# Staging the vector and scalar work of the second layer's feed-forward, one product step apart

## The chip, the cores and the metric

One core of one Trainium2 chip runs the whole program. TensorE (PE in the profile) does the matrix products, VectorE (DVE), ScalarE (ACT) and GpSimd (POOL) the element-wise work, SyncE's queue (SP) issues the weight loads. Each engine takes its instructions in the order in which the program wrote them and waits at any whose inputs are not there. The metric is the device time of one execution in microseconds (us).

## What is computed

A backbone of two layers over 512 tokens of width 1024, with 256 context tokens in front. Each layer mixes tokens in four branches and ends with a feed-forward part. The change is in the feed-forward part of the second layer, where only the 512 latent tokens are left:

```python
def sq_relu_mlp(h, w1, w2):          # w1: 1024 x 4096, w2: 4096 x 1024
    return jnp.square(jax.nn.relu(h @ w1)) @ w2
...
x = x + gt2 * sq_relu_mlp(h2, w_ff1[l], w_ff2[l])
...
return rmsnorm(x, g_final)
```

## The kernel before

**Products in two parts.** A 32-bit operand is split into a high part (a copy on ACT, rounded to the matmul's type) and a low part (source minus high part, on DVE or POOL); a product is three matmuls: high by high, high by low, low by high. `split` issues the copy (L344) and right behind it the subtraction (L345).

**Seven products.** w_ff1 is worked off in 16 quarters, each 1024 x 256. The first three are plain. For the other 13 (`seven`), the eight half-size block products are replaced by seven, P1 to P7, over sums of blocks. Per quarter that takes four weight sums on DVE (`seven_weights`: L294 and L296 for P6, L299 for P7, L308 for P3), a high and a low part per product, five adds that read the products' PSUM banks (L1451 to L1471), three rectifiers on ACT (L1461, L1467, L1473), and two squares (L1480), each followed by a split of the result. The sums on the side of the activations are made once, by the thread `sums` (adds and subtractions at L1405 and L1408 on DVE, then splits), which other work interleaves with.

**The product list.** `mixed` first runs `ff1_first` (the first four tiles of w_ff1, each followed by `act`: rectifier L1330 on ACT, square L1332 on DVE, split), then `ff_order`'s list of 149 steps: F, a plain w_ff1 tile (24 matmuls of 128x512, twice); S, one of the seven products (12 matmuls of 128x256, 91 times); a, one output tile of w_ff2 (12 matmuls of 128x512, 56 times; an odd a shares the weights of the even one before it). The list begins FFaaaSaSSaSaSaSSA (the capital A ends a group of eight a) and then repeats 14 S and 8 a for two quarters; FF_LEAD (5.6 us) sets how many products of the next quarters run ahead of the a steps. `ff2_last` follows with the last w_ff2 tiles and the final norm.

**What sets the order on DVE and ACT.** At each step `w_ahead` issues, ahead of the step's own matmuls, the loads of all weights due within LOAD_US = 12 us of the list's time and the sums and splits of those due within SPLIT_US = 6 us. `split`, the bank reads, the rectifier and the square are issued as soon as the code reaches them, right behind the matmuls that feed them. A tile whose number divides by `pool_share` has its low part on POOL (three in this stage).

Of the kernel before, what the change touches and what calls it, by code (L numbers as in the profile page):

```python
# [9 lines left out]
F32 = mybir.dt.float32  # L10
BF16 = mybir.dt.bfloat16
F32R = mybir.dt.float32r
# [54 lines left out]
SPLIT_US, LOAD_US, FF_LEAD = 6.0, 12.0, 5.6  # L67
# [49 lines left out]
class Net:  # L117
# [44 lines left out]
    def plan(self):  # L162
        d = self.d
        items = []
        self.when, self.sevens = {}, {}
# [22 lines left out]
        for l in range(DEPTH):  # L188
# [10 lines left out]
            if l in STRASSEN:  # L199
                t = 0.0  # L200
                for kind, a, b, us in self.ff_order(l):
# [6 lines left out]
                    self.when[items[-1][0]] = self.when.get(items[-1][0], t)  # L208
                    t += us
# [38 lines left out]
    def w_advance(self, dma, split):  # L248
# [8 lines left out]
        while self.n_split < min(split + 1, len(self.items)):  # L257
            i = self.n_split
            if self.items[i][0][0] == "seven":
                self.wsp[i] = self.seven_weights(i, *self.items[i][0][1:])  # L260
                self.n_split += 1
                continue
# [16 lines left out]
    def seven_weights(self, i, l, q, j):  # L279
# [35 lines left out]
        return w  # L315

    def w_ahead(self, *key):

        i = self.n_got
        now = self.when[key]  # L320

        def until(us):
            j = i
            while j + 1 < len(self.items) and self.when.get(self.items[j + 1][0], now + us + 1.0) <= now + us:
                j += 1
            return j

        split, load = max(until(SPLIT_US), i + 1), until(LOAD_US)
        self.n_got += 1
        assert self.items[i][0] == key, (self.items[i][0], key)  # L330
# [933 lines left out]
    def out(self, l, groups, x, h):  # L1264
# [6 lines left out]
        held = []  # L1271

# [11 lines left out]
        for m in range(KT):  # L1284
            xo = sb.get([128, NTOK], F32, "xo")
            nc.gpsimd.dma_start(xo[:, :n], self.x_src[m][:, :n])
            x.append(xo)
# [31 lines left out]
    def ff(self, l, ranges, groups, x, h, na, nb, after, near):  # L1319
# [17 lines left out]
        def ff1_first():  # L1337
# [6 lines left out]
            self.until(*nb, KT - 1)  # L1344
            hid = [act((b,), groups[:1]) for b in banks]
# [15 lines left out]
        def ff2_one(c, m, w, hid, rngs):  # L1361
            banks = self.proj(w, [256 * k + 128 * (m % 2) for k in range(4)], hid, rngs, "f2")
            for (a, e), o in zip(rngs, banks):
                nc.vector.scalar_tensor_tensor(x[m][:, a:e], o[:, :e - a], self.modcol(l, int(a >= SEQ), 5, m),  # L1364
                                               x[m][:, a:e], op0=OP.mult, op1=OP.add)
            ps.free(*banks)
# [30 lines left out]
        def sums():  # L1397

            blocks = {n: [] for n in ("T1", "T2", "T3", "T4")}
            keep = []  # L1400
            for k in range(4):
                v = sb.get([128, 4, 256], F32, "v7", ph=True)
                for i in range(2):
                    hi, lo = (t[:, :512].bitcast(F32).rearrange("p (a b) -> p a b", a=2) for t in h[k + 4 * i])
                    nc.vector.tensor_tensor(v[:, 2 * i:2 * i + 2], hi, lo, op=OP.add)  # L1405
                    yield 0.7
                for o, a, b in ((0, 1, 0), (1, 3, 1), (3, 3, 0), (2, 2, 3)):
                    nc.vector.tensor_tensor(v[:, o], v[:, a], v[:, b], op=OP.subtract)  # L1408
                yield 1.0
                t = sb.get([128, 2, 2, 256], F32R, "T7", ph=True)  # L1410
                keep.append(t)
                for n, i, (hi, lo) in (("T2", 3, [z[:, 512:] for z in h[4 + k]]), ("T3", 1, (t[:, 0, 0], t[:, 0, 1])),
                                       ("T1", 0, [z[:, 512:] for z in h[k]]), ("T4", 2, (t[:, 1, 0], t[:, 1, 1]))):
                    blocks[n].append(self.split(v[:, i], "T7", hi, lo))
                    yield 0.6
                sb.free(v)
# [5 lines left out]
        def seven(q, hid):  # L1422
# [5 lines left out]
            u = sb.get([128, 256], F32, "u7", ph=True)  # L1428

            def product(j):  # L1430
                n = SEVEN[j]
                w = self.w_ahead("seven", l, q, j)
# [13 lines left out]

            b1, o1 = product(0)
            nc.scalar.activation(u, o1, AF.Copy)
# [439 lines left out]
```

## Time and profile before

| | us |
|---|---|
| median of 3 runs | 2201.86 (2199.62 to 2201.98) |
| profiled execution | 2200.57 |
| its span, first to last instruction | 2198.8 |
| product list, first F to first matmul of `ff2_last` | 361.4 (1800.51 to 2161.92) |

The profile is of one execution. PE is busy for 96% of the span, DVE for 66%, ACT for 38%. The product list is 16% of the span; everything before it and the code after it are the same in both kernels. A timeline row gives start, duration, engine, line and operation, output tile <- input tiles, and in brackets the idle time of the engine just before it with the instruction that ended the wait. "x12" is a run of 12 equal instructions; matmuls overlap, so a run's pace is read from one row's start to the next. PEclk is the granted TensorE clock, 1.0 for 2.4 GHz and 0.5 for 1.2 GHz.

### The profile page before, as it was taken

Reading aid. Unit: us, or ns where it says so; the run is one execution under the profiler, and the core shown is the slowest. Engines: PE = TensorE matmul, PEld = TensorE weight load, DVE = VectorE, ACT = ScalarE, POOL = GpSimd, SP = SyncE. Lnnn points to the kernel's source line nnn. Section 1 sums busy time; section 2 is a strip of 40 time slices with the busy share of each in tenths; the row PEclk is TensorE's granted clock in tenths of the full one; section 3 lists DMA queues with packets and bytes.
Section 4 is the critical chain, followed back from the end, with each engine's and each line's share of the span. In section 5 each row is a group of like instructions: output and inputs, shape, how many; then the busy total and the mean of one; then the engine's idle time right before and its main releaser. Section 6 shows DMA issues by size and latency. Waiting matters only on the chain. (4 is left out here: it accounts for less than half of the span.)

```text
span 2198.8 us, 30361 instructions
## 1 busy us (share of the span) xinstructions
PE 2110.1 (96%) x12168; PEld 1829.9 (83%) x12168; DVE 1451.1 (66%) x2434; ACT 829.9 (38%) x1391; POOL 441.3 (20%) x387
## 2 busy tenths in 40 slices
PE   8899999999999999999999999999999997989988
PEld 6788888888888888888888888888888986777877
DVE  6667657689874668877333475767875577566566
ACT  3455542233432432122221245554423343343434
POOL 2432210025431322122000134332000130000000
PEclk9999999999999999999999999999999999999999
DMA  7111122133433144456221212223323321222222
GB/s 299 44 61 54 49 76 85 44 120 125 134 116 134 49 149 169 152 201 230 68 68 49 86 39 77 68 68 113 123 86 97 124 68 58 87 87 77 77 86 77
DMA packets 62173, 218.45 MB, mean 99 GB/s; under 512 B 7248, under 2 KB 9312, under 8 KB 62032
## 3 DMA queue, kind: packets, MB, share of 16 engines
q1 hardware_dynamic: 45136, 155.21, 21.4%
q0 software_dynamic: 16896, 61.30, 8.1%
q8 instruction: 95, 1.56, 0.3%
q14 instruction: 46, 0.38, 0.1%
HBM read 212.29 MB, written 4.19 MB: 98 GB/s over the span
## 5 line engine op out<-in xcount | busy, mean ns | idle before, releaser
L345 POOL TENSOR_TENSOR wl<-wraw,wh 128x1024 fp32r<-128x1024 f32 x86 | 211.5, 2460 | 1249.3 <-ACT wh L344 885.9
L364 PE MATMUL f<-fh,wh 128*128 128x512 f32 (+1 forms) x1040 | 289.2, 353 | 0.9 <-ACT fh L344 0.4
L344 ACT ACTIVATE wh<-wraw 128x1024 fp32r<-128x1024 f32 x242 | 249.5, 1048 | 48.4 <-DVE wl L345 23.1
L364 PE MATMUL f<-h,wh 128*128 128x256 f32 (+1 forms) x1184 | 257.7, 333 | 0.0
L364 PE MATMUL f<-fh,wl 128*128 128x512 f32 (+1 forms) x800 | 243.4, 349 | 6.9 <-DVE wl L345 3.5
L345 DVE TENSOR_TENSOR wl<-wraw,wh 128x1024 fp32r<-128x1024 f32 x156 | 202.5, 1304 | 32.7 <-ACT wh L344 30.9
L364 PEld LDWEIGHTS f<-h,wh 128*128 128x128 f32 x1184 | 184.7, 188 | 24.2
L1364 DVE SCALAR_TENSOR_TENSOR xo<-f,mod,xo 128x512 f32<-128x512 f32 (+1 forms) x200 | 122.8, 639 | 112.1 <-PE f L364 111.9
L364 PEld LDWEIGHTS f<-fh,wh 128*128 128x128 f32 x1040 | 173.3, 188 | 26.3 <-ACT fh L344 0.7
L425 DVE CUSTOM_DVE_ANT_0 junk<-wm,silu,pp 128x1024 bf16<-128x1024 f32 x116 | 157.7, 1360 | 12.3 <-DMA wm<-w_mod 11.0
L364 PE MATMUL f<-h,wl 128*128 128x512 f32 (+1 forms) x592 | 161.8, 335 | 0.0
L364 PE MATMUL g<-h,wh 128*128 128x512 f32 x512 | 161.6, 393 | 0.0
L364 PEld LDWEIGHTS f<-fh,wl 128*128 128x128 f32 x800 | 134.7, 188 | 30.4 <-DVE wl L345 5.7
L364 PE MATMUL f<-fl,wh 128*128 128x512 f32 (+1 forms) x560 | 155.2, 342 | 0.0
L364 PE MATMUL g<-hh,wh 128*128 128x512 f32 (+1 forms) x512 | 131.9, 338 | 0.0
L364 PE MATMUL g<-hh,wl 128*128 128x512 f32 (+1 forms) x512 | 131.3, 337 | 0.6 <-DVE wl L345 0.6
L364 PE MATMUL g<-hl,wh 128*128 128x512 f32 (+1 forms) x512 | 131.6, 338 | 0.0
L1330 ACT ACTIVATE ft<-f 128x512 f32<-128x512 f32 (+1 forms) x74 | 32.4, 477 | 247.8 <-PE f L364 247.8
L747 DVE SCALAR_TENSOR_TENSOR ca<-z,pp,ca 128x783 f32<-128x783 f32 (+1 forms) x120 | 121.0, 1008 | 1.9
L1186 ACT ACTIVATE g<-g 128x512 f32<-128x512 f32 x96 | 46.9, 523 | 194.2 <-PE g L364 193.3
L364 PE MATMUL y<-br,wh 128*128 128x512 f32 x480 | 119.6, 357 | 0.3 <-DVE br L345 0.2
L1441 PEld LDWEIGHTS f<-h,w 128*128 128x128 f32 x780 | 108.4, 206 | 12.8 <-ACT w L344 6.5
(430 smaller groups left out, 4419.0 us busy)
## 6 DMA issues: line engine op xcount, KB each, us to landing
wraw<-w_ff SPq DMA_DIRECT2D x128, 512.0 KB, 3.6
wraw<-w_in SPq DMA_DIRECT2D x96, 512.0 KB, 3.5
wm<-w_mod POOLq DMA_DIRECT2D x80, 512.0 KB, 4.5
wm<-w_mod SPq DMA_DIRECT2D x16, 512.0 KB, 10.2
wraw<-w_out SPq DMA_DIRECT2D x16, 512.0 KB, 3.6
wraw<-w_v SPq DMA_DIRECT2D x8, 512.0 KB, 5.7
bias<-bias POOLq DMA_DIRECT2D x16, 256.0 KB, 3.0
wraw<-w_ba SPq DMA_DIRECT2D x8, 512.0 KB, 3.6
```

The costliest lines, as they stand in the source:

```text
L344: nc.scalar.activation(hi, src, AF.Copy)
L345: (eng or nc.vector).tensor_tensor(lo, src, hi.bitcast(F32), op=OP.subtract)
L364: self.nc.tensor.matmul(o[:, :t1 - t0], a[:, sl], b[:, t0:t1], start=start and a is wh and b is xh, stop=stop and a is wl)
L425: nc.vector.tensor_tensor_reduce(self.junk, w, self.silu[c], 1.0, b, OP.mult, OP.add, o)
L747: nc.vector.scalar_tensor_tensor(a[:, :n], zs[ct][:, j:j + n], w, a[:, :n], op0=OP.mult, op1=OP.add)
L1186: nc.scalar.activation(g[:, a:e], o[:, :e - a], func, scale=scale)
L1330: nc.scalar.activation(t[:, a - a0:e - a0], o[:, :e - a], AF.Relu)
L1364: nc.vector.scalar_tensor_tensor(x[m][:, a:e], o[:, :e - a], self.modcol(l, int(a >= SEQ), 5, m), x[m][:, a:e], op0=OP.mult, op1=OP.add)
L1441: nc.tensor.matmul(o, y, x_, start=fresh and k + i == 0, stop=k == 3 and i == 2, skip_group_check=True)
```

## The change

The work around the products is put into stages that are issued at fixed distances on the product list:

- `schedule` replaces `w_ahead`. For the weights that step n uses it issues the DVE sums at step n-5, the ACT high part at n-4 and the DVE low part at n-3 (for a plain tile: the high part at n-4, the low part at n-3). The load is issued 6 us of the list's time ahead of step n-5. What would lie before step 0 is issued behind `ff1_first`, before the first F. POOL has no low parts here any more.
- Bank reads are issued one step behind their product, rectifiers two (the one over both halves of t1 becomes two of half the size), square and high part two behind that step, the low part three. The add of an a step into x (L1364, now L1391) is issued one step later.
- `sums` starts inside `ff1_first`, ahead of the first `act`, and issues the low parts of one round behind the sums of the next.
- FF_LEAD becomes 7.2 us: the list begins FFaaSaSaSaSaSSaSA, and the repeating part keeps its 14 S and 8 a.
- x of layer 2 is held as four pairs in wide buffers, in place of eight single ones; one tile (u) becomes a half of another.

```diff
-SPLIT_US, LOAD_US, FF_LEAD = 6.0, 12.0, 5.6
+STAGES_AHEAD, LOAD_US, FF_LEAD = 5, 6.0, 7.2
...
         name = SEVEN[j]
-        if name == "P1":
-            src = a
-        elif name == "P6":
+        if name == "P6":
             st["s1"], st["s2"] = (sb.get([128, 512], F32, "ws", ph=True) for _ in range(2))
             nc.vector.tensor_tensor(st["s1"], c, e, op=OP.add)
-            src = st["s2"]
-            nc.vector.tensor_tensor(src, st["s1"], a, op=OP.subtract)
+            nc.vector.tensor_tensor(st["s2"], st["s1"], a, op=OP.subtract)
         elif name == "P7":
-            src = c
-            nc.vector.tensor_tensor(src, a, c, op=OP.subtract)
-        elif name == "P5":
-            src = st["s1"]
-        elif name == "P2":
-            src = b
-        elif name == "P4":
-            src = e
-        else:
-            src = st["s1"]
-            nc.vector.tensor_tensor(src, b, st["s2"], op=OP.subtract)
+            nc.vector.tensor_tensor(c, a, c, op=OP.subtract)
+        elif name == "P3":
+            nc.vector.tensor_tensor(st["s1"], b, st["s2"], op=OP.subtract)
+        yield
+        src = dict(P1=a, P6=st.get("s2"), P5=st.get("s1"), P2=b, P3=st.get("s1"))[name] if name not in ("P7", "P4") else (
+            c if name == "P7" else e)
         w = sb.get([128, 2, 512], F32R, "w7", ph=True)
-        self.split(src, "w7", w[:, 0], w[:, 1])
+        nc.scalar.activation(w[:, 0], src, AF.Copy)
+        yield
+        nc.vector.tensor_tensor(w[:, 1], src, w[:, 0].bitcast(F32), op=OP.subtract)
...
+    def tile_weights(self, i):
+        nc, sb = self.nc, self.sb
+        yield
+        src = self.raw[i]
+        hi, lo = (sb.get([128, 1024], F32R, "w", ph=True) for _ in range(2))
+        nc.scalar.activation(hi, src, AF.Copy)
+        yield
+        nc.vector.tensor_tensor(lo, src, hi.bitcast(F32), op=OP.subtract)
+        sb.free(self.raw.pop(i))
+        self.wsp[i] = hi, lo
+    def schedule(self, steps, first):
+        due = {}
+        at, t = [], 0.0
+        for _, us in steps:
+            at.append(t)
+            t += us
+        i = first
+        for n, (key, _) in enumerate(steps):
+            if key is None:
+                continue
+            assert self.items[i][0] == key, (self.items[i][0], key)
+            m = n - STAGES_AHEAD
+            if i >= self.n_split:
+                gen = self.seven_weights(i, *key[1:]) if key[0] == "seven" else self.tile_weights(i)
+                for k in range(3):
+                    due.setdefault(m + k, []).append((k, lambda g=gen: next(g, None)))
+            start = at[m] if m >= 0 else m * 1.4
+            load = sum(1 for a in at if a <= start - LOAD_US) - 1 if start >= LOAD_US else -99
+            if i >= self.n_dma:
+                due.setdefault(load, []).append((-1, lambda i=i: self.load(i)))
+            i += 1
+        self.n_dma, self.n_split = max(self.n_dma, i), max(self.n_split, i)
...
-        self.w_advance(i, i)
-        self.w_advance(split, split)
-        self.w_advance(max(load, split + 1), split)
         return self.wsp.pop(i)
...
             self.until(*nb, KT - 1)
+            if l in STRASSEN:
+                threads.append(self.spawn(sums()))
             hid = [act((b,), groups[:1]) for b in banks]
...
+            add = lambda o, x: lambda: nc.vector.tensor_tensor(o, x, u, op=OP.add)
+            copy = lambda o, x, f: lambda: nc.scalar.activation(o, x, f)
+            free = lambda *t: lambda: ps.free(*t)
             b1, o1 = product(0)
-            nc.scalar.activation(u, o1, AF.Copy)
+            defer(1, copy(u, o1, AF.Copy))
             yield
             b6, o6 = product(1)
-            nc.vector.tensor_tensor(u, o6, u, op=OP.add)
-            ps.free(b6)
+            defer(1, add(u, o6), free(b6))
             yield
             b7, o7 = product(2)
-            nc.vector.tensor_tensor(t1[:, 1], o7, u, op=OP.add)
+            defer(1, add(t1[:, 1], o7))
             yield
             b5, o5 = product(3)
-            nc.vector.tensor_tensor(t1[:, 1], o5, t1[:, 1], op=OP.add)
+            defer(1, lambda: nc.vector.tensor_tensor(t1[:, 1], o5, t1[:, 1], op=OP.add))
+            defer(2, copy(t1[:, 1], t1[:, 1], AF.Relu))
             yield
             product(4)
-            nc.scalar.activation(t0[:, 0], o1, AF.Relu)
-            ps.free(b1)
+            defer(1, copy(t0[:, 0], o1, AF.Relu), free(b1))
             yield
             product(5)
-            nc.vector.tensor_tensor(t1[:, 0], o7, u, op=OP.add)
-            ps.free(b7)
-            nc.scalar.activation(t1, t1, AF.Relu)
+            defer(1, add(t1[:, 0], o7), free(b7))
+            defer(2, copy(t1[:, 0], t1[:, 0], AF.Relu))
             square(t1, hid[1])
...
         def square(t, hl):
             f = t.rearrange("p a b -> p (a b)")
-            nc.scalar.activation(f, f, AF.Square)
-            self.split(f, "f", hl[0], hl[1])
+            hi, lo = hl
+            defer(2, lambda: nc.scalar.activation(f, f, AF.Square), lambda: nc.scalar.activation(hi, f, AF.Copy))
+            defer(3, lambda: nc.vector.tensor_tensor(lo, f, hi.bitcast(F32), op=OP.subtract), lambda: sb.free(t))
...
             hid = ff1_first()
-            t7 = self.spawn(sums())
+            order = self.ff_order(l)
+            keys = [("ff1", l, a) if kind == "plain" else ("seven", l, a, b) if kind == "seven" else
+                    ("ff2", l, a, b // 2) if b % 2 == 0 else None for kind, a, b, _ in order]
+            due = self.schedule([(key, s[3]) for key, s in zip(keys, order)] +
+                                [(("ff2", l, 7, j), 24 * SEQ / 2217.0) for j in range(2)], self.n_got)
+            for n in [n for n in due if n < 0]:
+                for f in due.pop(n):
+                    f()
             nxt, gen = [], None
-            for kind, a, b, _ in self.ff_order(l):
+            for n, ((kind, a, b, _), key) in enumerate(zip(order, keys)):
+                now[0] = n
+                for f in later.pop(n, ()):
+                    f()
+                for f in due.pop(n, ()):
+                    f()
...
```

Two places in the instruction order. **ACT, around the end of `ff1_first`**: `ft` rows are rectifiers, `fh` high parts of activations, `h`/`T` high parts of the block sums `v`, `wh`/`w ... 128x1024` the high part of a plain weight tile; f_1451 is the last bank of `ff1_first`, wraw_15718 (before) and wraw_15714 (after) the weights of the second F. Before:

```order
L1330 ACTIVATE ft_16032<-f_1451_16007 128x256
L344 ACTIVATE fh_15910<-ft_16032 128x256
L344 ACTIVATE wh_16037<-wraw_15718 128x1024
L344 ACTIVATE h_15611<-v_3314_16045 128x256
L344 ACTIVATE T_3315_16070<-v_3314_16045 128x256
```

and after:

```order
L1353 ACTIVATE ft_15991<-f_1447_15955 128x256
L361 ACTIVATE fh_15892<-ft_15991 128x256
L1444 ACTIVATE h_15609<-v_3297_15977 128x256
L1444 ACTIVATE T_3303_16015<-v_3297_15977 128x256
L1444 ACTIVATE h_15601<-v_3297_15977 128x256
L1444 ACTIVATE T_3303_16015<-v_3297_15977 128x256
L1353 ACTIVATE ft_16026<-f_1449_15996 128x256
L361 ACTIVATE fh_15899<-ft_16026 128x256
L1353 ACTIVATE ft_16067<-f_1451_16031 128x256
L361 ACTIVATE fh_15906<-ft_16067 128x256
L309 ACTIVATE w_16078<-wraw_15714 128x1024
L309 ACTIVATE w_16082<-wraw_15716 128x1024
```

The second F's high part stood right behind the last rectified tile of `ff1_first`, ahead of every row of block sums. It now stands behind two rounds of them (eight rows), whose inputs come from DVE.

**DVE, in the repeating part**, where one quarter ends and the next begins: `ws` and `wraw<-wraw` rows are weight sums, `w` their low parts, `ft` bank reads, `fh` low parts of activations, `xo` the adds of a steps. Before:

```order
L345 TENSOR_TENSOR w_3869_18507<-wraw_18459,w_3869_18507 128x512
L294 TENSOR_TENSOR ws_18510<-wraw_18461 128x512
L296 TENSOR_TENSOR ws_18511<-ws_18510,wraw_18459 128x512
L345 TENSOR_TENSOR w_3872_18514<-ws_18511,w_3872_18514 128x512
L1471 TENSOR_TENSOR ft_18317<-f_1631_18423,u_3840_18319 128x256
L345 TENSOR_TENSOR fh_18314<-ft_18317,fh_18313 128x512
L1364 SCALAR_TENSOR_TENSOR xo_15477<-f_1639_18536,mod_103,xo_15477 128x512
L299 TENSOR_TENSOR wraw_18461<-wraw_18459,wraw_18461 128x512
```

and after:

```order
L285 TENSOR_TENSOR ws_18474<-wraw_18424 128x512
L286 TENSOR_TENSOR ws_18475<-ws_18474,wraw_18387 128x512
L1482 TENSOR_TENSOR ft_18317<-f_1626_18372,ft_18316 128x256
L297 TENSOR_TENSOR w_3843_18472<-wraw_18387,w_3843_18472 128x512
L288 TENSOR_TENSOR wraw_18424<-wraw_18387,wraw_18424 128x512
L1391 SCALAR_TENSOR_TENSOR xo_15443<-f_1636_18497,mod_103,xo_15443 128x512
L297 TENSOR_TENSOR w_3847_18492<-ws_18475,w_3847_18492 128x512
L1516 TENSOR_TENSOR fh_18315<-ft_18317,fh_18314 128x512
```

Before, the low part w_3872 stood one row behind the sum ws_18511 that it is taken from, and fh_18314 one row behind the bank read of its own tile. After, the low part of ws_18475 stands five rows behind its sum, and other products' rows are in between.

## Rows read from the trace of the kernel before

**Rows 1.** Page, part 1: engine, busy us, share of the span, instructions:

```profile
PE 2110.1 (96%) x12168; PEld 1829.9 (83%) x12168; DVE 1451.1 (66%) x2434; ACT 829.9 (38%) x1391; POOL 441.3 (20%) x387
```

**Rows 2.** Stretches: busy us (instructions) of PE, PEld, DVE, ACT, POOL; PEclk; DMA:

```profile
1800.50:1839.20 38.70, 30.34 (x135) 24.75 (x134) 32.70 (x62) 16.01 (x33) 0.00 (x0) 0.91 0.14 43
1839.20:2161.90 322.70, 291.69 (x1680) 255.98 (x1680) 193.75 (x299) 126.49 (x213) 7.09 (x3) 0.95 0.26 84
2161.90:2198.80 36.90, 27.97 (x223) 26.55 (x221) 23.76 (x65) 15.89 (x31) 4.42 (x6) 0.98 0.20 72
```

**Rows 3.** PE waits, 1800.5 to 2162: total us, times, longest us:

```profile
PE f L1441 <- ACT w L344: 28.5, 13, 6.0
PE f L1441 <- DVE w L345: 3.7, 10, 1.7
```

**Rows 4.** Timeline of PE in the repeating part of the list:

```profile
2064.88 3.23 PE L1441 MATMUL f<-T,w 128*128 128x256 f32 x12 [3.20 <-ACT w L344]
2067.91 4.47 PE L1441 MATMUL f<-h,w 128*128 128x256 f32 x24
...
2075.00 1.60 PE L1441 MATMUL f<-T,w 128*128 128x256 f32 x12
2076.44 0.63 PE L364 MATMUL f<-fh,wh 128*128 128x512 f32 x2
...
2079.23 3.04 PE L1441 MATMUL f<-h,w 128*128 128x256 f32 x24
...
2116.00 3.23 PE L1441 MATMUL f<-T,w 128*128 128x256 f32 x12 [3.19 <-ACT w L344]
```

**Rows 5.** Stretches, as Rows 2, of 5.8 us at the start:

```profile
1833.40:1839.20 5.80, 5.79 (x25) 5.57 (x26) 4.71 (x7) 3.62 (x6) 0.00 (x0) 0.51 0.01 3
```

**Rows 6.** Timeline of DVE ahead of the PE stall at 2064.88:

```profile
2057.94 0.69 DVE L296 TENSOR_TENSOR ws<-ws,wraw 128x512 f32<-128x512 f32 x1
2059.33 0.69 DVE L345 TENSOR_TENSOR w<-ws,w 128x512 fp32r<-128x512 f32 x1 [0.70 <-ACT w L344]
...
2062.16 0.69 DVE L345 TENSOR_TENSOR fh<-ft,fh 128x512 fp32r<-128x512 f32 x1 [1.81 <-ACT fh L344]
...
2063.43 0.68 DVE L299 TENSOR_TENSOR wraw<-wraw,wraw 128x512 f32<-128x512 f32 x1
```

**Rows 7.** Timeline of ACT at the same place:

```profile
2064.20 0.63 ACT L344 ACTIVATE w<-wraw 128x512 fp32r<-128x512 f32 x1 [2.07 <-DVE wraw L299]
```

**Rows 8.** Timeline of PE at the start of the list:

```profile
1800.51 0.62 PE L364 MATMUL f<-h,wh 128*128 128x512 f32 x2
...
1806.09 0.62 PE L364 MATMUL f<-h,wh 128*128 128x512 f32 x2
...
1833.41 3.23 PE L1441 MATMUL f<-h,w 128*128 128x256 f32 x12 [6.02 <-ACT w L344]
```

**Rows 9.** Timeline of DVE at the start of the list:

```profile
1794.54 0.43 DVE L345 TENSOR_TENSOR fl<-ft,fh 128x256 fp32r<-128x256 f32 x1 [0.55 <-ACT fh L344]
...
1795.86 0.42 DVE L345 TENSOR_TENSOR fl<-ft,fh 128x256 fp32r<-128x256 f32 x1 [0.55 <-ACT fh L344]
...
1803.04 1.23 DVE L345 TENSOR_TENSOR wl<-wraw,wh 128x1024 fp32r<-128x1024 f32 x1 [0.53 <-ACT wh L344]
1804.18 1.29 DVE L1405 TENSOR_TENSOR v<-h,h 128x512 f32<-128x512 f32 x2
1805.39 1.80 DVE L1408 TENSOR_TENSOR v<-v 128x256 f32<-128x256 f32 x4
```

**Rows 10.** Timeline of ACT at the start of the list:

```profile
1801.96 1.04 ACT L344 ACTIVATE wh<-wraw 128x1024 fp32r<-128x1024 f32 x1
1806.76 0.42 ACT L344 ACTIVATE h<-v 128x256 fp32r<-128x256 f32 x1 [3.75 <-DVE v L1408]
```

**Rows 11.** Weight loads of the list (L254), issue to landing:

```profile
DMA to landing us min/median/max: 3.3/3.6/5.5
```

**Rows 12.** Timeline of PE in `ff2_last`:

```profile
2163.26 0.38 PE L364 MATMUL f<-fh,wh 128*128 128x256 f32 x1 [0.45 <-ACT fh L344]
```

More of the change, by code (lines that the diff above doesn't have):

```diff
@@ L164, in plan @@
         items = []
-        self.when, self.sevens = {}, {}
+        self.sevens = {}
         def win(l, m):
@@ L199, in plan @@
             if l in STRASSEN:
-                t = 0.0
-                for kind, a, b, us in self.ff_order(l):
+                for kind, a, b, _ in self.ff_order(l):
                     if kind == "plain":
@@ L314, in seven_weights @@
             sb.free(st["raw", 0], st["s1"], st["s2"])
-        return w
-    def w_ahead(self, *key):
-        i = self.n_got
[L320 to L328, printed above, removed]
+        self.wsp[i] = w
+    def tile_weights(self, i):
[8 more added lines that the diff above has]
+        self.wsp[i] = hi, lo
@@ L329, in w_ahead, with load, w_next @@
+    def load(self, i):
+        if self.items[i][1] is not None:
+            t = self.sb.get([128, self.items[i][2]], F32, "wraw", True)
+            self.nc.sync.dma_start(t, self.items[i][1])
+            self.raw[i] = t
+    def w_next(self, key):
+        i = self.n_got
+        assert self.items[i][0] == key, (self.items[i][0], key)
         self.n_got += 1
-        assert self.items[i][0] == key, (self.items[i][0], key)
-        self.w_advance(i, i)
-        self.w_advance(split, split)
@@ L1359, in ff1, with ff2_one, add @@
             return hid
-        def ff2_one(c, m, w, hid, rngs):
+        def ff2_one(c, m, w, hid, rngs, later=False):
             banks = self.proj(w, [256 * k + 128 * (m % 2) for k in range(4)], hid, rngs, "f2")
[L1363 to L1366, printed above, removed]
+            def add():
+                for (a, e), o in zip(rngs, banks):
+                    nc.vector.scalar_tensor_tensor(x[m][:, a:e], o[:, :e - a], self.modcol(l, int(a >= SEQ), 5, m),
+                                                   x[m][:, a:e], op0=OP.mult, op1=OP.add)
+                ps.free(*banks)
+            return add if later else add()
         def ff2(c, hid):
@@ L1399, in sums @@
             blocks = {n: [] for n in ("T1", "T2", "T3", "T4")}
-            keep = []
+            keep, low = [], []
             for k in range(4):
@@ L1470, in seven @@
             product(6)
-            nc.vector.tensor_tensor(t0[:, 1], o5, u, op=OP.add)
-            ps.free(b5)
-            nc.scalar.activation(t0[:, 1], t0[:, 1], AF.Relu)
+            defer(1, add(u, o5), free(b5))
+            defer(2, copy(t0[:, 1], t0[:, 1], AF.Relu))
             square(t0, hid[0])
-            sb.free(u, t0, t1)
             yield
@@ L1500, in mixed @@
                 else:
[L1501 to L1503 removed]
+                    if key:
+                        w2 = self.w_next(key)
+                    done = ff2_one(a, b, w2, hid, ranges, True)
+                    defer(1, done)
                     if b % 2:
@@ L1509, in mixed @@
                         hid, nxt = nxt, []
+            for fs in [due.pop(n) for n in sorted(due)] + [later.pop(n) for n in sorted(later)]:
+                for f in fs:
+                    f()
             for t in h:
@@ L1515, in ff @@
         self.pool_share = SHARES[2 + l]
-        x7 = {}
+        x7, now, threads = {}, [0], []
         if l in STRASSEN:
@@ L1736, in after @@
                     if g == 1:
-                        gen = self.chain(gen, self.drop(ssq, last, *x))
+                        gen = self.chain(gen, self.drop(ssq, last, *self.x_tiles))
                     norms.append(self.spawn(gen))
```

49 lines of the change are left out of this document (28 added, 21 removed).

## Prediction

> **What bounds the kernel now.** I read the page's engine line first: PE is busy for 96% of the span [rows 1], so time can come back only where PE stands still or runs slowly. Next the view by stretches over the product list, 1800.5 to 2161.9 [rows 2]: PE is busy for 30.34 of 38.70 us and then for 291.69 of 322.70, so it is idle for 39.4 us, and the granted clock is 0.91 and 0.95. DVE (193.75 us of the longer stretch) and ACT (126.49) are far from full: what holds PE is an order, not an engine that is too slow. PE's waits say which [rows 3]: 28.5 us in 13 stalls for ACT's high part of a product's weights, 3.7 us for DVE's low part.
>
> How much the list could take without them comes from PE's own pace. An F took 1806.09 - 1800.51 = 5.58 us [rows 8]; an S 2076.44 - 2075.00 = 1.44; an a 2079.23 - 2076.44 = 2.79 [rows 4]. Two F, 56 a and 91 S are 11.16 + 156.24 + 131.04 = 298.4 us. The list takes 361.4, so 63.0 us are lost: 39.4 idle, and 23.6 in matmuls at the lower clock. That second part follows the long stalls. After the 3.20 us stall at 2064.88, three S and one a took until 2075.00, 10.12 us for 7.11 us of work, 3.0 lost [rows 4]; after the 6.02 us stall at 1833.41 [rows 8] the granted clock was 0.51, the 1.2 GHz level, over the next 5.8 us [rows 5]. A long stall costs its length and about 3 us more.
>
> By place: up to 1839.2 the list has done FFaaaSaSS, 11.16 + 4 x 2.79 + 3 x 1.44 = 26.6 us of work in 38.7, so 12.1 are lost at the start. Of the repeating part, 2064.88 to 2116.00 is 51.12 us for 14 S and 8 a (42.5 us), 8.6 lost, and it ends at a stall of 3.19 us at the same kind of product as the one of 3.20 with which it began [rows 4]. The 13 quarters are 6.5 such parts; they and what lies between hold the other 50.9 us.
>
> The timelines show how such a stall comes about. DVE ended a weight sum (2057.94), then waited 0.70 for ACT's high part before the low part of that same sum (2059.33) and 1.81 more for ACT's high part of an activation (2062.16); only then came the next product's sum, at 2063.43 [rows 6]. ACT had waited 2.07 us for that sum and began the copy at 2064.20 [rows 7], and PE, which waited for the copy, went on at 2064.88 [rows 4]. Both engines wait for each other in turns, because each result is asked for one row behind its source, and weights begun 6 us ahead come late.
>
> **The change part by part.** *Weights in stages.* The sums, the high part and the low part of a product are now issued five, four and three steps ahead of it, with other products' rows between. DVE's work is nearly the same: 193.75 us plus three low parts of 1.23 [rows 9] that POOL made, 197.4 us, against 298.4 - 26.6 = 271.8 us of PE work in that stretch, 73%; ACT's 126.5 us are 47%. Laid out by the order of the changed kernel with the durations above, the fullest list step gives DVE about 2.4 us (a sum pair, a bank read, a low part). Three steps are at least 3 x 1.44 = 4.3 us, so one full step doesn't reach PE; two in a row would be made up by the a steps that follow. I therefore expect the 13 stalls of the repeating part to go, and with them the slow matmuls behind them: 50.9 us, of which I leave 1.5 as an estimate for small waits of the sort that Rows 3 shows for DVE (0.37 each).
>
> *Reads one step later.* An add that reads a bank now stands ahead of the next step's matmuls and waits on DVE for the product before to end; behind it queue that step's sums and low parts. They are meant for products three and five steps on, so a wait of up to a step (1.44 to 2.79 us) hides there. If that cover failed, it would show as PE waits for DVE's low parts. Banks are held a step longer; in the order of the changed kernel at least four of eight are still free at each product, and the one taken is the longest free. I cost this at nothing.
>
> *The rectifier in two halves* adds some 0.2 us to ACT per quarter, 2.7 us in all at 47% load: nothing. *Three low parts from POOL to DVE* are in the 73%. *x in pairs* moves no instruction of the list: nothing.
>
> *Loads.* They are issued 6 us of list time ahead of the first stage, not 12 ahead of use. The tightest are w_ff2 tiles behind five S: 6 + 5 x 1.44 = 13.2 us from issue to use, less the high part (1.04, [rows 10]), the low part (1.23) and about 0.2 for the hand-overs, leaves 10.7 for a load; these landed in 3.6, at most 5.5 us [rows 11]. Nothing.
>
> *The start gets worse.* This is the one place where the change puts work ahead of PE. The second F's high part stood right behind the last tile of `ff1_first` and ran at 1801.96 [rows 10], with its low part at 1803.04 [rows 9], in time for 1806.09. Now block sums stand ahead of it on both engines. From the rows: the first four activation tiles end on DVE at 1796.2 (the row at 1795.86); a round of sums is 1.2 + 1.8 = 3.0 us (1804.18 to the end of the row at 1805.39); an activation tile takes 1.32 (1794.54 to 1795.86), or some 2.4 where its rectifier queues behind a round's four copies on ACT, the first of which comes 1.37 us after the subtractions start (1806.76 against 1805.39); four low parts of a round some 1.4 (0.42 each, overlapping) [rows 9, 10]. In the new order: round 0 (3.0), tile 0 (2.5), round 1 (3.0), low parts 0 (1.4), tile 1 (1.3), tile 2 (2.4), round 2 (3.0), low parts 1 (1.4), tile 3 (1.3): 19.3 us, to 1815.5. ACT copies the second F's high part from about 1814.9 to 1815.9, DVE its low part to 1817.2. PE, done with the first F at 1811.67 - 5.58 = 1806.1, stands for about 10 us, then loses 2.9 at the lower clock: F two ends near 1825.2 in place of 1811.67 at full pace, 13.5 lost. Before, the start lost 12.1; those stalls (S0's and S2's weights) go, since the weights behind are early by then: by the same walk the low part of S0 ends near 1825.3 and is wanted at 1830.8.
>
> *The end.* `ff2_last` waits 0.45 us for an activation's high part [rows 12]; the chain behind the last product is the same, so I leave it (0 to 0.5 gained).
>
> *Sum.* The list: 298.4 + 13.5 + 1.5 = 313.4 us, 48.0 less than 361.4. The profiled execution's span becomes 2198.8 - 48.0 = 2150.8; outside the span lie 2200.57 - 2198.8 = 1.8, so 2152.6; the median of the runs is 1.3 above that execution: 2153.9, rounded to **2154 us**, 2.2% less. Bounds of the terms: start loss 6 (tiles of `ff1_first` pass quicker) to 18 us; small waits 0 to 10.
>
> **The rivals.** *Still late once per repeating part.* DVE waits in order for bank reads, and the parts with six S in a row give it two products' sums and reads in 8.6 us. If PE met one unready weight there, each time long enough for the lower clock (0.5 + 3.0 us), 6.5 parts cost 23 us: 2177. For it: 73% load in bursts, with 0.7 us from a sum over ACT back to DVE [rows 6]. Against: three steps of slack, and no DVE row there that waits for a source from its own step.
>
> *Buffers, not order.* If the gaps that repeat came from tiles waiting for space, the high part's copy would wait until a product still to run gave up its buffer. Staging holds more tiles at once, the lead would shrink to what it is, and 8.6 us would be lost per part as now: 2202, within 4 us. The Trainium skill (Perfetto Trace Analysis, Optimization Strategy) says that consistent bubbles on the engine that should be saturated can mean that there isn't enough SBUF or PSUM for the next tile. By that rule this is the reading, and the change does nothing. The trace names others: ACT waited 2.07 us for DVE's sum, and DVE for ACT [rows 6, 7], so I give it little.
>
> *Slower: loads come late.* Lead was cut, and SP's queue issues a load only when the buffer that it fills is free. From a landing (with that wait) of 10.7 us on, each of the 28 w_ff2 tiles would stop PE; at 12.5 us that is 28 x 1.8 = 50 us, which eats the gain, and with 3 us of lower clock each it is 134: 2204 to 2288, about 2220 with the clock lost at every fifth. Against it: 5.5 us at most now [rows 11].
>
> **How the numbers follow.** Forecast, 2143 to 2163: 0.77. The start much shorter than walked, under 2143: 0.04. Late once per part, 2163 to 2190: 0.12. Buffers: 0.04. Late loads: 0.03. The range leaves out the lowest case, the last two and the upper half of the second: 2143 to 2170, 0.83 inside. A measurement of this kernel can tell 0.2%, 4.4 us, from no change. Faster by more: 0.77 + 0.04 + 0.12 = 0.93; within: 0.04; slower: 0.03.
>
> **What would show it.** In the profile after: PE's wait for ACT's high parts in S down from 28.5 us to a few; one wait of about 10 us for the second F's high part near 1816, with a clock near 0.5 behind it; the clock at 1.0 and a part of 14 S and 8 a in 42.5 to 43 us from there on; DVE rows of low parts that wait for nothing; loads landing in 3 to 6 us. Wrong would be: stalls of the S rows at regular places (first rival), ACT copies that wait for PE (second), or waits for the loads (third); or a start whose second F begins at 1806, with the sums' rows late instead.

## The result

The changed kernel takes 2147.87 us (median of 4 runs, 2145.32 to 2150.55) against 2200.74 for the kernel before beside it: a ratio of 0.9762, 95% interval 0.9745 to 0.9779. The forecast was 2154 us, with a range of 2143 to 2170.

The profiled execution took 2145.32 us, its span 2143.5. The page of the changed kernel, part 1, which answers to [rows 1]; then the same stretches as in [rows 2], cut at the new ends of the start and of the list (columns as there), with one more for the 5.8 us behind the long stall, which answers to [rows 5]:

```profile
PE 2082.6 (97%) x12168; PEld 1814.2 (85%) x12168; DVE 1448.5 (68%) x2437; ACT 832.7 (39%) x1404; POOL 435.7 (20%) x384
```

```profile
1800.80:1822.50 21.70, 13.93 (x51) 10.39 (x50) 17.59 (x40) 8.02 (x19) 0.00 (x0) 0.76 0.09 27
1822.50:2108.00 285.50, 285.50 (x1766) 256.52 (x1765) 203.38 (x324) 139.23 (x242) 0.00 (x0) 1.00 0.32 100
2108.00:2143.50 35.50, 27.32 (x223) 26.34 (x221) 22.81 (x64) 14.19 (x29) 4.43 (x6) 0.95 0.17 60
```

```profile
1814.30:1820.10 5.80, 5.74 (x14) 4.08 (x15) 5.70 (x10) 3.13 (x7) 0.00 (x0) 0.58 0.00 0
```

In the 285.5 us from the end of the second F to the end of the list PE is busy for all of them, at a clock of 1.00. All that is left to lose lies in the first 21.7 us. PE's waits in the list, which answer to [rows 3], and its timeline in the repeating part, which answers to [rows 4]:

```profile
PE f L381 <- ACT w L309: 7.7, 1, 7.7
PE f L381 <- DVE fh L1516: 0.6, 1, 0.6
```

```profile
1968.66 1.60 PE L1476 MATMUL f<-h,w 128*128 128x256 f32 x12
...
2010.90 1.60 PE L1476 MATMUL f<-h,w 128*128 128x256 f32 x12
```

The 28.5 us of waits for ACT's high parts in S are gone, and a part of 14 S and 8 a takes 2010.90 - 1968.66 = 42.24 us (51.12 before). The 0.6 us is in `ff2_last` and answers to [rows 12]. The list itself, from the first F to the end of its last step, took 361.4 us before and takes 307.2 now; 296.7 would be without any loss (11.2 for the two F and 285.5 as above). The start, which answers to [rows 8 to 10], on PE, its weight loads (PEld), ACT and DVE:

```profile
1800.81 0.64 PE L381 MATMUL f<-h,wh 128*128 128x512 f32 x2
...
1814.32 8.26 PE L381 MATMUL f<-h,w 128*128 128x512 f32 x24 [7.73 <-ACT w L309]
1822.41 0.40 PE L381 MATMUL f<-fh,w 128*128 128x512 f32 x1
```

```profile
1815.57 6.57 PEld L381 LDWEIGHTS f<-h,w 128*128 128x128 f32 x22 [0.76 <-DVE w L311]
```

```profile
1813.22 1.99 ACT L309 ACTIVATE w<-wraw 128x1024 fp32r<-128x1024 f32 x2
```

```profile
1794.47 0.43 DVE L362 TENSOR_TENSOR fl<-ft,fh 128x256 fp32r<-128x256 f32 x1 [0.55 <-ACT fh L361]
...
1813.35 0.43 DVE L362 TENSOR_TENSOR fl<-ft,fh 128x256 fp32r<-128x256 f32 x1 [0.48 <-ACT fh L361]
1814.30 2.36 DVE L311 TENSOR_TENSOR w<-wraw,w 128x1024 fp32r<-128x1024 f32 x2 [0.52 <-ACT w L309]
```

The second F waits 7.73 us for its high part and then takes 8.09 us in place of 5.58, in a stretch with a clock of 0.58; its weight loads wait another 0.76 us for the low part. Loss at the start: 1822.41 - 1800.81 - 11.16 = 10.4 us. The loads of the list, which answer to [rows 11]:

```profile
DMA to landing us min/median/max: 3.3/3.5/5.0
```

### The profile page after: what moved, and what is told of

It reads as the page before. It is cut to its first block, busy times and chain, and to the rows that moved or that the text cites. A ratio compares the mean times of both kernels' runs of the same rounds, so it can differ in the third digit from the quotient of the medians.

```text
span 2143.5 us, 30360 instructions
## 1 busy us (share of the span) xinstructions
PE 2082.6 (97%) x12168; PEld 1814.2 (85%) x12168; DVE 1448.5 (68%) x2437; ACT 832.7 (39%) x1404; POOL 435.7 (20%) x384
## 5 line engine op out<-in xcount | busy, mean ns | idle before, releaser
L362 POOL TENSOR_TENSOR wl<-wraw,wh 128x1024 fp32r<-128x1024 f32 x83 | 204.7, 2468 | 917.0 <-ACT wh L361 643.8
L361 ACT ACTIVATE wh<-wraw 128x1024 fp32r<-128x1024 f32 x211 | 217.2, 1049 | 46.1 <-DVE wl L362 23.1
L1391 DVE SCALAR_TENSOR_TENSOR xo<-f,mod,xo 128x512 f32<-128x512 f32 (+1 forms) x200 | 123.1, 640 | 130.6 <-PE f L381 130.4
L362 DVE TENSOR_TENSOR wl<-wraw,wh 128x1024 fp32r<-128x1024 f32 x128 | 168.5, 1323 | 28.4 <-ACT wh L361 26.5
L381 PE MATMUL f<-fh,w 128*128 128x512 f32 (+1 forms) x720 | 173.4, 379 | 0.6 <-DVE fh L1516 0.6
L381 PE MATMUL f<-fh,wh 128*128 128x512 f32 (+1 forms) x576 | 148.0, 331 | 0.0
L381 PEld LDWEIGHTS f<-fh,w 128*128 128x128 f32 x720 | 126.6, 188 | 23.8 <-DVE fh L1516 0.8
L381 PE MATMUL f<-fh,wl 128*128 128x256 f32 (+1 forms) x544 | 145.3, 334 | 0.0
L381 PE MATMUL f<-fl,wh 128*128 128x512 f32 (+1 forms) x512 | 136.3, 337 | 0.0
L381 PEld LDWEIGHTS g<-h,wh 128*128 128x128 f32 x512 | 96.0, 188 | 20.9 <-issue 0.5
```

The costliest lines, as they stand in the source:

```text
L361: nc.scalar.activation(hi, src, AF.Copy)
L362: (eng or nc.vector).tensor_tensor(lo, src, hi.bitcast(F32), op=OP.subtract)
L381: self.nc.tensor.matmul(o[:, :t1 - t0], a[:, sl], b[:, t0:t1], start=start and a is wh and b is xh, stop=stop and a is wl)
```

## Experiments

Up to `ff1_first` the code is the same in all kernels, yet the first F began anywhere from 1799.4 to 1805.7 us in the fourteen profiles. So I compare the length of the list, from the start of the first F to the start of the last S plus 4.2 us (that S and the a behind it), and the median with its ratio to the kernel before, run beside it.

| kernel | list, us | median, us | ratio (95% interval) |
|---|---|---|---|
| before | 361.4 | 2200.74 | 1 |
| changed | 307.2 | 2147.87 | 0.9762 (0.9745 to 0.9779) |
| e1_reads_at_once | 307.1 | 2149.35 | 0.9768 (0.9754 to 0.9783) |
| e2_back_to_back | 307.6 | 2149.36 | 0.9768 (0.9753 to 0.9782) |
| e3_ahead3 | 316.3 | 2156.62 | 0.9800 (0.9786 to 0.9815) |
| e7_lead12_18 | 309.7 | 2150.68 | 0.9776 (0.9759 to 0.9792) |
| e7_lead9_12 | 322.0 | 2163.22 | 0.9832 (0.9818 to 0.9845) |
| e7_buffers | 360.3 | 2201.91 | 1.0011 (1.0002 to 1.0020) |
| e9_load1 | 307.4 | 2148.34 | 0.9765 (0.9751 to 0.9778) |
| e5_sums_late | 308.2 | 2149.93 | 0.9775 (0.9762 to 0.9789) |
| e8_fill | 307.3 | 2148.65 | 0.9769 (0.9756 to 0.9782) |
| e6c_start | 302.3 | 2145.10 | 0.9751 (0.9738 to 0.9764) |
| e6e_start | 305.2 | 2145.91 | 0.9757 (0.9744 to 0.9770) |
| e6f_start | 297.3 | 2136.81 | 0.9712 (0.9698 to 0.9725) |

### Distance or lead: four runs

The forecast said that PE waited because each result was asked for one row behind its source, and that putting other rows between cures it. The first run takes that away for the activations:

```diff
         def defer(n, *fs):
-            later.setdefault(now[0] + n, []).extend(fs)
+            for f in fs:
+                f()
```

> The changed kernel (2147.9 us) with the rectifiers, squares, high and low parts of the activations and the adds issued at once behind their product, as before the change; the weights stay in their three stages. Order theory (what cost time was a result asked for one row behind its source): DVE waits again about 1.8 us for ACT at each of the two activation low parts of a quarter, 26 x 1.8 = 47 us, so its load goes from 197 to some 245 of 272 us; with weights three steps ahead PE sees little of it: 2148 to 2158 us. Rival (the lead of the weights is all): 2148. Rival (the deferral of reads is what counts): most of the 53 us comes back, near 2190.

The second takes it away for the weights: sum, high part and low part in a row at step n-4.

```diff
-                for k in range(3):
-                    due.setdefault(m + k, []).append((k, lambda g=gen: next(g, None)))
+                due.setdefault(m + 1, []).append((1, lambda g=gen: [next(g, None) for _ in range(3)]))
```

> The changed kernel with the sum, high part and low part of a weight issued one behind the other at step n-4, in place of n-5, n-4 and n-3: the lead is kept, the distance between the three is taken away. Order theory: each of 119 low parts makes DVE wait about 0.7 us for ACT, 83 us on top of 197, which is more than the 272 us that PE needs there; stalls come back in every repeating part: 2165 to 2185 us. Rival (an earlier start is all that was needed): 2148.

Both lists are as short as the changed kernel's (307.1 and 307.6), and the medians lie within each other's scatter. PE's waits in the lists of e1 and of e2:

```profile
PE f L381 <- ACT w L309: 8.2, 1, 8.2
```

```profile
PE f L380 <- ACT w L309: 7.7, 1, 7.7
```

That is the second F alone. The DVE waits came back, as the order has it. DVE's waits of the changed kernel, of e1 and of e2, each from near 1825 to the end of the list (total us, times, longest):

```profile
DVE xo L1391 <- PE f L381: 61.7, 52, 2.3
DVE ft L1482 <- PE f L1476: 13.3, 14, 1.6
```

```profile
DVE fh L1516 <- ACT fh L1515: 45.3, 25, 1.8
DVE xo L1391 <- PE f L381: 27.7, 21, 1.7
```

```profile
DVE w L297 <- ACT w L295: 43.9, 52, 1.6
DVE xo L1390 <- PE f L380: 29.6, 20, 2.1
```

In the changed kernel DVE waits for PE, 75 us and more. In e1 it waits 45.3 us for ACT and in e2 43.9, and what it waits for PE shrinks by about as much. PE sees nothing of that. For e1 I had expected 47 us of such waits, and little of them on PE; for e2 83 us and stalls from them, and that expectation fell.

The third run goes the other way: the kernel before, with its order of instructions within a split and its reads at once, and only more lead. Lead needs buffers for the tiles that are under way, so x in pairs had to come with it; without it the program has no free buffers for a lead of even 8 us, and lead without them wasn't tried.

```diff
-SPLIT_US, LOAD_US, FF_LEAD = 6.0, 12.0, 5.6
+SPLIT_US, LOAD_US, FF_LEAD = 12.0, 18.0, 5.6
...
+                if m % 2 == 0:
+                    self.x_tiles.append(sb.get([128, 2, SEQ], F32, "xo"))
+                x.append(self.x_tiles[-1][:, m % 2])
```

> The kernel before (2200.7 us) with x in pairs (which frees buffers) and its weights begun 12 us ahead (loads 18) in place of 6 and 12; the order within a split and the reads stay as they were. Order theory: DVE still waits for ACT one row behind each source, 78 us in the middle stretch of the kernel before (8.7 + 3.3 + 18.2 + 48.1), so with 194 us of work it needs about as long as PE; some of the stalls go, many stay: 2175 to 2200 us. Rival (lead is all): 2148 to 2160. Rival (buffers were short): the freed buffers alone already give several per cent of the list, under 2190.

Its ratio, 0.9776, is that of the changed kernel within the intervals; the 2175 to 2200 us that I expected if the order decides were not met. DVE's waits in the middle stretch of the kernel before, then in the same part of this run, and the stretch behind this run's start (columns as in [rows 2]):

```profile
DVE fh L345 <- ACT fh L344: 48.1, 25, 2.0
DVE xo L1364 <- PE f L364: 45.3, 21, 4.1
DVE w L345 <- ACT w L344: 26.9, 37, 0.8
```

```profile
DVE fh L345 <- ACT fh L344: 48.1, 25, 2.0
DVE w L345 <- ACT w L344: 26.7, 37, 0.8
DVE xo L1370 <- PE f L364: 1.9, 3, 1.1
```

```profile
1845.00:2108.00 263.00, 262.97 (x1638) 236.47 (x1638) 182.45 (x291) 123.27 (x210) 7.54 (x3) 1.00 0.31 100
```

The waits for ACT are the same to 0.2 us (48.1 and 26.9 against 48.1 and 26.7), and PE has no stall in 263 us, at a clock of 1.00. So with this lead the waits cost PE nothing: they are idle time of an engine that has some to spare. In the kernel before, where the weights are begun 6 us ahead of use, the same chain through DVE's and ACT's queues ended too late for PE [rows 4, 6, 7]. That a longer lead is enough doesn't show that order does nothing at the short one; the run with three stages ahead, below, bears on that. DVE has little left in this form, though: 189 us of work and 77 of waits for ACT in 272 us.

How much lead is needed, with the same kernel at 9 and 12:

```diff
-SPLIT_US, LOAD_US, FF_LEAD = 6.0, 12.0, 5.6
+SPLIT_US, LOAD_US, FF_LEAD = 9.0, 12.0, 5.6
```

> The kernel before with x in pairs and weights begun 9 us ahead (loads 12, as before). Lead theory: the stalls in the repeating part were 3.2 us long, so 3 us more of lead leaves next to none of them, while DVE goes on waiting 77 us for ACT: 2150 to 2160 us. Rival (DVE is nearly full with these waits, so a lead only pushes its backlog on): about half of the gain, near 2175.

Neither number was met: 2163.2 us, 36.5 us less than the kernel before, about 70% of the changed kernel's gain. PE's waits in its list:

```profile
PE f L1447 <- ACT h L344: 6.8, 2, 3.8
PE f L1447 <- ACT u L1454: 6.7, 6, 1.7
PE f L1447 <- DVE w L345: 0.9, 4, 0.2
```

The first row is the start (the block sums, which e7_lead12_18 waits for too, 8.3 us). The second is new: product P2 adds on to P1's bank and must wait until ACT has read P1 from it; that read now queues behind high parts on ACT (two rows of ACT and the row of PE at one such P2):

```profile
1864.92 1.04 ACT L344 ACTIVATE wh<-wraw 128x1024 fp32r<-128x1024 f32 x1
1865.87 0.36 ACT L1454 ACTIVATE u<-f 128x256 f32<-128x256 f32 x1
```

```profile
1866.28 2.71 PE L1447 MATMUL f<-h,w 128*128 128x256 f32 x12 [1.75 <-ACT u L1454]
```

Weights are hardly what comes last any more (0.9 us in the third row).

### Buffers alone

The lead run above has two edits; this one has x in pairs alone.

```diff
+                if m % 2 == 0:
+                    self.x_tiles.append(sb.get([128, 2, SEQ], F32, "xo"))
+                x.append(self.x_tiles[-1][:, m % 2])
```

> The kernel before (2200 us) with x in pairs, which frees buffers, and nothing else; it splits the run before with the longer lead into its two edits. Lead theory: no PE wait was for a buffer, so nothing changes: 2197 to 2202 us, list 361 us. Rival (buffers were short, as consistent bubbles can mean): under 2190.

Nothing is gained: 360.3 us of list, ratio 1.0011, and PE's longest row of waits is the one of [rows 3]:

```profile
PE f L1447 <- ACT w L344: 27.9, 13, 5.9
```

PE's waits stayed what they were. The loads' queue (SPq) does wait for the buffers that it fills, here as in the kernel before; its longest row, from 1840 to 2160:

```profile
SPq L254 <- PE f L364: 130.6, 19, 9.6
```

But in either list only one of ACT's copies waited for a load, 0.4 us, and none of DVE's rows did. Buffers still set how much lead the program can hold: neither the 12 us of the lead run nor the five steps of the changed kernel have room without the pairs, which do nothing alone. The three steps of the next run have room without them, in a form that was not run.

### How much slack the stages have

```diff
-STAGES_AHEAD, LOAD_US, FF_LEAD = 5, 6.0, 7.2
+STAGES_AHEAD, LOAD_US, FF_LEAD = 3, 6.0, 7.2
```

> The changed kernel with the stages at n-3, n-2 and n-1 in place of n-5, n-4 and n-3. Order theory with the slack as I walked it: the fullest step gives DVE 2.4 us, one step of S gives PE 1.44, so a low part one step ahead comes up to 1 us late in some steps, with lower clock where the wait is long: 2150 to 2170 us. Rival (the distance alone counts, the lead does not matter): 2148.

8.7 us slower than the changed kernel, inside what was expected, and by small waits. PE's own waits show 0.9 us of them; the view of the weight loads (PEld) shows the rest:

```profile
PEld f L381 <- DVE w L311: 11.8, 22, 1.0
```

```profile
1825.00:2114.00 289.00, 286.79 (x1736) 251.01 (x1737) 200.42 (x319) 133.47 (x234) 0.00 (x0) 1.00 0.31 97
```

22 low parts of w_ff2 tiles came up to 1.0 us late, 11.8 us in all; the list is 9.1 us longer. The second fence is the stretch behind the start (columns as in [rows 2]): PE counts as busy for nearly all of it and the clock is 1.00, so these waits cost no more than themselves.

This run also shows what the order is worth where the lead is short. Three steps are 3 x 1.44 = 4.3 us at least, and 3 x 42.24 / 22 = 5.8 at the mean of the repeating part, so that the sums are begun about as late as in the kernel before (within 6 us of use), and the low parts are asked for later than there. Yet its list takes 316.3 us against 361.4, 45 of the changed kernel's 54 us, and less than the 322.0 of the old order with 9 us of lead. So one of the two is enough for most of the gain: the old order with 12 us of lead, or the staged form with about 6. The staged form here holds the other parts of the change too (late reads, FF_LEAD, the early sums, no low parts on POOL); which of them count at the short lead wasn't separated.

Loads, 1 us ahead of the first stage in place of 6:

```diff
-STAGES_AHEAD, LOAD_US, FF_LEAD = 5, 6.0, 7.2
+STAGES_AHEAD, LOAD_US, FF_LEAD = 5, 1.0, 7.2
```

> The changed kernel with each load issued 1 us of list time ahead of the first stage in place of 6: 8.2 us from issue to use for the tightest tile, less 2.5 for high and low part, against a landing of 3.6 (5.5 at most). Forecast's slack: DVE or ACT wait up to 2 us for a load at some tiles, PE for none: 2147 to 2151 us. Rival (loads decide): stalls at the w_ff2 tiles, 2160 us or more.

The list is 307.4 us: PE waits for the second F as in the changed kernel and for nothing behind it. Loads had slack to spare.

### The start

Block sums back at their old place, behind `ff1_first`:

```diff
-            if l in STRASSEN:
-                threads.append(self.spawn(sums()))
...
             hid = ff1_first()
+            threads.append(self.spawn(sums()))
```

> The changed kernel with the block sums started behind the first four tiles, where they stood before the change. Start theory: the 7.7 us wait for the second F's high part, and the 2.5 us that its 24 matmuls lose at the lower clock, come from the block sums ahead of it; without them F two runs on time, but the sums then end later than the first product that reads them (P6, wanted at about 1821.7; sums ready near 1828 to 1830): a wait of 6 to 8 us with 2.5 of lower clock there. Net 2145 to 2150 us, the wait moved from F two to P6. Rival (the start is bound by something else, such as the loads): F two waits as long as now.

The list is 308.2 us. The wait moved, as expected, but in parts: in place of 6 to 8 us at P6, PE waits 2.2 us at the first w_ff2 tile, 1.1 for the weights of a product and 4.0 for the sums:

```profile
1822.24 0.84 PE L381 MATMUL f<-fh,w 128*128 128x512 f32 x2 [2.19 <-DVE w L311]
...
1827.76 0.86 PE L1474 MATMUL f<-h,w 128*128 128x256 f32 x5 [1.13 <-DVE w L297]
1832.27 1.01 PE L1474 MATMUL f<-h,w 128*128 128x256 f32 x3 [3.65 <-DVE h L1443]
```

The clock's part by itself: 33 matmuls of no use between the two F fill the wait.

```diff
                     banks = self.proj(w, K8, h, ranges, "f1")
+                    if n == 0:
+                        junk = self.bank("f1")
+                        for i in range(33):
+                            nc.tensor.matmul(junk[:, :512], w[0][:, 128 * (i % 8):128 * (i % 8) + 128], h[i % 8][0][:, :512], start=i == 0, stop=i == 32, skip_group_check=True)
+                        ps.free(junk)
```

> The changed kernel with 33 more matmuls of 128x512 between the two F, of no use to the output, into a spare bank: 7.7 us of PE work in the place of the 7.7 us wait. Clock theory: F two then runs at 2.4 GHz, 5.6 us for its 24 matmuls in place of 8.1, and the list ends 2.5 us earlier: 2145.4 us, if the filler doesn't outlast the wait. Rival (F two was slow because its low parts came late, 1815.5): its 24 matmuls take some 6.5 us or more, under 1.5 us gained.

```profile
1811.26 7.82 PE L1546 MATMUL f<-h,wh 128*128 128x512 f32 x33
1819.68 0.73 PE L381 MATMUL f<-h,w 128*128 128x512 f32 x2 [0.60 <-ACT w L309]
1820.93 5.29 PE L381 MATMUL f<-h,w 128*128 128x512 f32 x22 [0.53 <-DVE w L311]
1826.06 0.40 PE L381 MATMUL f<-fh,w 128*128 128x512 f32 x1
...
1834.78 0.72 PE L381 MATMUL f<-fh,w 128*128 128x512 f32 x2 [1.05 <-DVE w L311]
```

With PE kept busy the last 22 matmuls of the F take 1826.06 - 1820.93 = 5.13 us, 0.233 each, the pace of the first F (5.58 / 24). All 24 take 1826.06 - 1819.68 = 6.38, not the 5.6 expected, since the third waits 0.53 us for the low part; in the changed kernel they took 8.09. Of the 2.5 us that were lost there, the clock's share is thus 1.7, and 0.8 is the low part's, which was the rival. The time was not gained: measured from the first F, the second ended 1.2 us earlier than in the changed kernel (20.4 against 21.6), and a wait of 1.05 us for the next w_ff2 tile (the row at 1834.78) took that back.

So I moved the work. First, block sums ahead of the third tile of `ff1_first`, and a first group that asks for them later:

```diff
+            ahead = FF_LEAD if l not in STRASSEN or c > 1 else 1.0
...
-                while b and (ta - FF_LEAD) / (total - FF_LEAD) > (tb + 6 * us) / more:
+                while b and (ta - ahead) / (total - ahead) > (tb + 6 * us) / more:
...
+            for j, (w, hl) in enumerate(zip(ws, hid)):
+                if l in STRASSEN and j == 2:
+                    threads.append(self.spawn(sums()))
```

> The changed kernel with the block sums started ahead of the third of the first four tiles, and the first group of the list reordered to FaaFaaSaSSaSSaSSa, so that the products that read the sums come later. Start theory: the first a waits 3 to 5 us for its weights (high part near 1810, wanted 1806.4) with about 2 us of lower clock, P6 little: start loss 6 to 8 in place of 10.4, 2143 to 2146 us. Rival (DVE's total work before P6 decides, in any order): 2148.

and the same with `j == 3`:

> As the run before, but the block sums start ahead of the fourth tile. Start theory: the first a waits under 1 us; P6 waits near 6 us (its low part near 1833.8, wanted 1827.8) with 2.5 of lower clock: start loss 8 to 10, 2145 to 2148 us. Rival (DVE's total work decides): 2148.

The lists are 302.3 and 305.2 us, start losses of 5.6 and 8.5. In e6c the first a waits 2.26 us for its high part (3 to 5 expected); in e6e that is nearly gone, and a later w_ff2 tile, not P6 as expected, waits 5.40:

```profile
1809.02 0.50 PE L382 MATMUL f<-fh,w 128*128 128x512 f32 x1 [2.26 <-ACT w L310]
```

```profile
1833.27 1.22 PE L382 MATMUL f<-fh,w 128*128 128x512 f32 x2 [5.40 <-DVE w L312]
```

In both DVE's queue ahead of the first products is what PE waits for, so the last version also takes work off it: the squares in `act` go to ACT, F two's split goes ahead of `ff1_first`'s tiles, and both F lead the list (FFaaaaSaSSaSSaSSa).

```diff
-            nc.vector.tensor_tensor(t, t, t, op=OP.mult)
+            if l in STRASSEN:
+                nc.scalar.activation(t, t, AF.Square)
+            else:
+                nc.vector.tensor_tensor(t, t, t, op=OP.mult)
...
             hid = [act((b,), groups[:1]) for b in banks]
+            if l in STRASSEN:
+                self.w_advance(self.n_got + 1, self.n_got + 1)
...
+            if c == 1 and l in STRASSEN:
+                out.sort(key=lambda s: s[0] != "plain")
```

> The changed kernel with a new start: the second F's weights are split ahead of the tiles of ff1_first, the block sums start ahead of the third of them, the squares of these tiles and of the two F go from DVE to ACT, and the first group is FFaaaaSaSSaSSaSSa. Start theory: F two and the first a run on time, DVE ends the sums near 1825, the third w_ff2 tile is some 1.5 us late: start loss 1 to 4 us in place of 10.4, list 298 to 301 us, 2139 to 2143 us. Rival (DVE's total work before P6 decides, in any order): 2145 or more.

2136.81 us, ratio 0.9712: 11 us under the changed kernel and 2 under the range expected. The whole list of this run as one stretch:

```profile
1799.40:2096.70 297.30, 297.18 (x1815) 265.65 (x1814) 216.93 (x356) 148.90 (x264) 0.00 (x0) 1.00 0.31 97
```

PE is busy for 297.18 of 297.30 us at a clock of 1.00. The start, which cost 12.1 us before and 10.4 in the changed kernel, costs 0.6. Which of the three edits over e6c brings how much wasn't separated.

## Why the prediction held, and where it did not

**The size held.** The list was forecast at 313.4 us and took 307.2. The terms: start 13.5 forecast, 10.4 measured; small waits 1.5, none measured; and the pace, 287.3 us for 56 a and 91 S taken from single rows, 285.5 measured, since the two rows that I took lie at the slow end. The code behind the list took 1.4 us less than before (35.5 against 36.9), where I had left 0 to 0.5. In the median 1.2 us of this are hidden again: it lies 2.5 above the profiled execution, not 1.3.

**The start was walked rightly but from a late point.** I let DVE's first four tiles end at 1796.2; they ended at 1794.82, behind the row at 1794.47. From there to the end of tile 3 the walk had 19.3 us and the rows have 18.9 (1794.82 to about 1813.7). So PE stood for 7.7 us and not for about 10. The lower clock was put at 2.9 us and cost about 1.7; the late low part cost 0.8. The forecast named no cost for that one, though 0.6 of its 13.5 lies beyond the stand and the clock (10 and 2.9).

**The reason given for the repeating part names two things, and as far as these runs show it takes both to cost PE its time.** "Both engines wait for each other in turns, because each result is asked for one row behind its source" is true of DVE's rows, and the text took these waits for the cause of PE's. The lead run keeps every one of them, and PE's stalls are gone; the two runs that bring them back into the changed kernel cost nothing that can be measured. So the waits alone are not the cause. Nor is the lead alone, "weights begun 6 us ahead come late": with the stages and about that lead, e3's list is 9 us longer than the changed kernel's, and the old order's is 54 longer. The old order with 12 us gives all of the gain in the repeating part, with 9 us 70% of the whole. The change made both cures at once, either of which would have brought most of the gain, and the forecast could be right without telling them apart. At five steps the stages leave DVE about 75 us of slack behind PE in the list, which nothing in this kernel uses.

**"x in pairs moves no instruction of the list: nothing"** is right for the edit alone (1.0011) and wrong for its part in the change, since the five steps don't fit without it. The rival that went by the Trainium skill (Perfetto Trace Analysis, Optimization Strategy), that consistent bubbles can mean too little SBUF or PSUM, fell in the form in which I priced it: buffers alone change nothing, and PE's stalls are gone. Its sign did appear, small and without effect: six of ACT's copies in the changed kernel wait for PE, 1.9 us at most, and PE waits for none of them.

```profile
ACT w L295 <- PE f L1476: 11.0, 6, 1.9
```

In another form buffers are part of the story, because what ran out was room for more lead when the program was laid out, and no row of these traces names that as a wait.

**Slack, loads, end.** The first rival, one unready weight per part, has no row: behind the second F PE waits for no weight in the list. One step of slack in place of three costs 8.7 us, as the walk of 2.4 us in the fullest step against 1.44 said, so three steps were enough and one is not. The rival of late loads fell by a wide margin: loads land as before, 3.5 us at the median and 5.0 at most, and 5 us less lead changes nothing. `ff2_last` still waits 0.6 us.

## What to carry to other kernels

When the bound engine waits at regular places for a result that two others pass back and forth, first ask how early that chain is begun, and whether there are buffers to begin it earlier; waits between the two helpers cost nothing while the chain is early enough and they have time to spare. Where there is no room for more lead, look at the order: staging the links of the chain at about the old lead brought 45 of the 54 us here. Only runs that change lead and order one at a time tell the two apart. Then look at the first microseconds of the stage, where a steady schedule has no lead yet: here another order there, with some of DVE's work moved to ACT, was worth another 10 us.

## What had not been expected of the hardware

A late low part can hide from PE's own row of waits: in e3 PE shows 0.9 us of waits and is busy nearly throughout, while the weight loads show 11.8 us. The clock was 0.58 behind the changed kernel's stall of 7.73 us, and 0.56 over the 2.5 us behind the wait of 1.75 us in e7_lead9_12, but 1.00 through the 22 waits of e3 (1.0 us at most); with matmuls of no use in place of the long stall it was 1.00, and the pace 0.233 us each.
